# Seven block products in both layers' FFN, and one layer's modulation moved from VectorE to TensorE

## The chip, the cores and the metric

The kernel runs on one core of a Trainium2 chip. Its time is the device time of one execution in microseconds (us); 1701.05 is the median of three runs (1700.99 to 1702.76). The profile comes from one more execution, of 1706.92 us.

## The reference

Two layers work on 512 latent tokens and 256 context tokens of width 1024, in fp32. Each layer modulates its normed input, projects it, runs four head groups side by side (gated spatial mixing, a bidirectional mLSTM, windowed attention, pooling), projects out, adds; then the same with a gated FFN of hidden width 2816. Context tokens are dropped after layer 0's FFN and the keys, values and states that layer 1 takes from them.

```python
def trunk_layer(x, ctx, c, c_ctx, ...):
    sh_a, sc_a, g_a, sh_f, sc_f, g_f = split(silu(c) @ w_mod + b_mod, 6)      # context: the same of c_ctx
    zx = modulate(rms_norm(x, norm_g[0]), sh_a, sc_a) @ w_in
    mix_x, mix_c = token_mixers(zx, zc, ...)
    x = x + g_a * rms_norm(mix_x @ w_out, norm_g[1])
    x = x + g_f * rms_norm(swiglu(modulate(rms_norm(x, norm_g[2]), sh_f, sc_f), w_ffn_in, w_ffn_out), norm_g[3])

def swiglu(h, w_in_, w_out_):
    gate, up = split(h @ w_in_, 2)
    return (silu(gate) * up) @ w_out_
```

## The kernel before

**Products in three matmuls.** Activations lie as 8 tiles of 128 features by tokens. Every fp32 operand is split into a high half (`split`, L401 to L409: a copy on ScalarE, L405) and a low half (a subtraction on VectorE or GpSimd, L406), and a product is three matmuls (`mac3`, L464 to L466): high by high, high by low, low by high.

**Weights.** `weights` (L411) takes one unit: a load of up to 512 KB on SyncE's queue into the ring `wr` (5 slots), then the split into `wh` and `wl` (5 slots each). A `wr` slot is free again when its last reader is done; a load waits in the queue for its slot, and later loads wait behind it.

**Order.** Python emits the program in order, and a list scheduler with a cost model sets each engine's own order at build time, earlier emitted work first. Some work is emitted a piece at a time: modulation pieces stand in a list `bg`, and each `weights` call adds `bg_rate` to an account and emits a piece when it reaches 1 (`tick`); `flush` emits what is left.

**Modulation.** A layer has six parts of 1024 by 1024. `mods` (L603) does a part in four pieces of two row blocks: it loads two raw tiles of 512 KB into `wr`, runs four matmuls (each two instructions, L628) whose stationary operand is 128 x 32, each into another group of 32 columns of the array, and adds the result into a row buffer (VectorE, L631, L634); four transposes (L639) end a part. `mods_sums` (L653) does the same for latent tokens alone as weighted sums over rows on VectorE (L669, L671) into `macc`, and eight small matmuls with a vector of ones per half part (L677). Layer 0's parts 2 to 5 go by `mods` in layer 0's input projection, layer 1's parts 0 and 1 by `mods` during the context's FFN, and layer 1's parts 2 to 5 by `mods_sums` during layer 0's FFN (L1904).

**FFN.** The hidden width is 22 blocks of 128. A pair is block j of the gate and of the up weights; a chunk of pairs gives activations `g` (`gh`, `gl`), which an output tile per 128 features (`ffn_tiles`, L1602) multiplies by its block of `w_ffn_out` and adds to `y` (L1450). The first three pairs and the last output tiles run in two halves of 256 tokens, so that norms can overlap. Layer 0 (`ffn`, L1665) does all pairs dense: 2 x 8 matmul triples of 512 tokens. Layer 1 (`ffn_seven`, L1611) does 4 pairs dense and 18 by seven block products (Strassen's scheme in Winograd's form): the input's four quarters give sums (`strassen_rhs`, L1507), the pair's weights as a 2 by 2 block matrix give sums in the ring `ws` (`strassen_pair`, L1535, sums at L1547), and seven products of 4 triples with 256 tokens each, summed on the way out of PSUM, give gate and up. The output tiles of one chunk are emitted between the products of the next.

**Around it.** After layer 0's first three pairs, the context's states are computed, and the arena slots of the context are given to the latent tokens (`mix` in `run`). Layer 1's input projection is emitted by `order` from the string `l1`: first `in_halves`, then tiles between steps of the mLSTM (`m`), then attention (`a`).

Of the kernel before, what the change touches and what calls it, by code (L numbers as in the profile page):

```python
# [11 lines left out]
F32 = mybir.dt.float32  # L12
# [5 lines left out]
ALU = mybir.AluOpType  # L18
# [3 lines left out]
P = 128  # L22
D = 1024
KT = D // P
# [12 lines left out]
T = {'ntmp': 5,  # L37
 'netmp': 3,
 'nmain': 36,
 'nctx': 26,  # L40
 'wr': 5,
 'wh': 5,
 'wl': 5,
 'fcx': ((0, 8), (8, 15), (15, 22)),
 'fcc': ((0, 4), (4, 8), (8, 12), (12, 16), (16, 19), (19, 22)),
# [18 lines left out]
 'latei': 2,  # L64
 'rate0': 0.8,
 'rate1': 0.2,
 'rate2': 0.5,
 'lo': ('4', '4', '6', '3', '2', '4', '5', '3', '4'),
 'sqk': 'VPVPVPVP',
 'sqe': 'AAAAAAAA',  # L70
# [35 lines left out]
 'cbc': 's',  # L106
 'pom': '2310',
 'por': '1023',
 'strassen': (1,),
 'fcs': ((0, 4), (4, 8), (8, 12), (12, 15), (15, 22)),  # L110
 'sad': 'PPVV',
 'slo': 'PVVPPVP',
 'sre': 'VPVP',
# [1 line left out]
 'srl': 'VPVP',  # L115
 'sup': 'V',
 'sgl': 'V',
 'ws': 6}
UNIT = 1024
HALF = 544  # L120
NEG = -1e30
# [139 lines left out]
class Build:  # L261
    def __init__(self, tc, es, I, out, dbg=None):
        self.tc, self.nc, self.I, self.out, self.dbg = tc, tc.nc, I, out, dbg
        pool = lambda name, **k: es.enter_context(tc.tile_pool(name=name, **k))
        self.cp = pool("const", bufs=1)
        self.pp = pool("param", bufs=1)
        self.sp = pool("small", bufs=1)
        self.wr = pool("wr", bufs=T["wr"])
        self.wh = pool("wh", bufs=T["wh"])
        self.wl = pool("wl", bufs=T["wl"])  # L270
        self.ws = pool("ws", bufs=T["ws"])
        self.ap = pool("arena", bufs=1)
        self.dr = pool("dram", bufs=1, space=bass.MemoryType.DRAM)
        self.pmm = pool("pmm", bufs=4, space=PSUM)
        self.pmx = pool("pmx", bufs=3, space=PSUM)
        self.pms = pool("pms", bufs=1, space=PSUM)
        self.main = Arena(self.ap, "m", T["nmain"])
        self.side = Arena(self.ap, "c", T["nctx"])
        self.main.other, self.side.other = self.side, self.main
        self.tmp = Arena(self.ap, "t", T["ntmp"])  # L280
        self.etmp = Arena(self.ap, "e", T["netmp"])
        self.ar = self.main
        self.modrow = Arena(self.sp, "modrow", 1)
        self.bg = deque()
        self.pre = deque()
        self.bg_rate = self.bg_acc = 0.0
        self.uid = 0
        self.fine = False
        self.ph = 0
        self.lo_i = 0  # L290
        self.cpy_i = 0
# [116 lines left out]
            nc.scalar.activation(hi, src, AF.Copy, scale=scale)  # L408
            nc.vector.scalar_tensor_tensor(out=lo, in0=src, scalar=scale, in1=hi.bitcast(F32), op0=ALU.mult, op1=ALU.subtract)  # L409

    def weights(self, src, shape, hold=False):  # L411

        nc = self.nc
        if self.pre:
            return self.pre.popleft()
        self.tick()
        nk, m = shape
        raw = self.wr.tile([P, UNIT], F32, tag="wr", name=self.name("wr"))
        nc.sync.dma_start(out=raw[:, 0:nk * m].rearrange("p (a b) -> p a b", a=nk), in_=src)
        w = Stream()  # L420
        w.h, w.l, w.slots = [], [], []
        per = max(1, HALF // m)
        for a in range(0, nk, per):
            k = min(per, nk - a)
            if hold:
                w.slots += [self.ar.get("wt", F32R), self.ar.get("wt", F32R)]
                hi, lo = w.slots[-2].t, w.slots[-1].t
            else:
                hi = self.wh.tile([P, HALF], F32R, tag="wh", name=self.name("wh"))
                lo = self.wl.tile([P, HALF], F32R, tag="wl", name=self.name("wl"))  # L430
            self.lo_i += 1
            self.split(hi[:, 0:k * m], lo[:, 0:k * m], raw[:, a * m:(a + k) * m], eng=nc.gpsimd if self.lo_pool() else None)
            w.h += [hi[:, i * m:(i + 1) * m] for i in range(k)]
            w.l += [lo[:, i * m:(i + 1) * m] for i in range(k)]
        w.free = lambda: [x.free() for x in w.slots]
        return w
# [166 lines left out]
    def mods(self, l, parts, p, ahead=False):  # L603
# [44 lines left out]
        for part in parts:  # L648
            box = []
            for k0 in range(0, KT, 2):  # L650
                self.bg.append(lambda part=part, k0=k0, box=box: pair(part, k0, box))

    def mods_sums(self, l, parts, p, streams):  # L653

        nc = self.nc
        p.mod = getattr(p, "mod", None) or self.pp.tile([P, 48, 2], F32, tag=f"mod{l}", name=f"mod{l}")

        def pair(part, i, k0, acc):
            raw = self.wr.tile([P, UNIT], F32, tag="wr", name=self.name("wr"))
            c = slice(i * 512, i * 512 + 512)  # L660
            nc.sync.dma_start(out=raw.rearrange("p (k c) -> p k c", k=2), in_=self.I["wmod"][l, part, k0:k0 + 2, :, c].rearrange("k p c -> p k c"))
            if k0 == 0:
                acc += [self.main.get("macc") for _ in range(streams)]
            for k in (k0, k0 + 1):
                w = raw[:, (k - k0) * 512:(k - k0) * 512 + 512]
                for s in range(streams):
                    t = acc[s].t[:, 0:512]
                    if k == 0:
                        nc.vector.tensor_scalar(out=t, in0=w, scalar1=self.cs[:, k, s:s + 1], scalar2=1.0, op0=ALU.mult, op1=ALU.mult)  # L669
                    else:  # L670
                        nc.vector.scalar_tensor_tensor(out=t, in0=w, scalar=self.cs[:, k, s:s + 1], in1=t, op0=ALU.mult, op1=ALU.add)  # L671
            if k0 < KT - 2:
                return
            ps = self.ms()
            for s in range(streams):
                for b in range(4):
                    nc.tensor.matmul(ps[:, s * 4 + b:s * 4 + b + 1], acc[s].t[:, b * P:(b + 1) * P], self.ones[:, 0:1], start=True, stop=True)  # L677
                acc[s].free()
            o = part * 8 + i * 4
            for s in range(streams):  # L680
                nc.vector.tensor_tensor(out=p.mod[:, o:o + 4, s], in0=ps[:, s * 4:s * 4 + 4], in1=p.bmod[:, o:o + 4], op=ALU.add)

        for part in parts:
            for i in range(2):
                acc = []
                for k0 in range(0, KT, 2):
                    self.bg.append(lambda part=part, i=i, k0=k0, acc=acc: pair(part, i, k0, acc))

    def mod_col(self, p, l, s, kind):

# [844 lines left out]
    def strassen_pair(self, l, j, h, rhs, g, jj):  # L1535

        nc = self.nc
        n = h.half
# [4 lines left out]
            nc.sync.dma_start(out=r.rearrange("p (a b) -> p a b", a=KT), in_=self.I["wfi"][l, j, u])  # L1543
            raw.append(r)
        a11, a12, a21, a22 = raw[0][:, 0:512], raw[0][:, 512:1024], raw[1][:, 0:512], raw[1][:, 512:1024]
        s = [self.ws.tile([P, 512], F32, tag="ws", name=self.name("ws")) for _ in range(4)]
        tt = lambda c, o, a, b, op: self.e(c).tensor_tensor(out=o, in0=a, in1=b, op=op)  # L1547
        ad = T["sad"]
        tt(ad[0], s[0], a21, a22, ALU.add)
        tt(ad[1], s[2], a11, a21, ALU.subtract)  # L1550
        tt(ad[2], s[1], s[0], a11, ALU.subtract)
        tt(ad[3], s[3], a12, s[1], ALU.subtract)
        lhs = [a11, a12, s[1], s[0], s[2], s[3], a22]
        z, w, y = self.mm(), None, None
        c1 = self.ar.temp("fc", 2 * n)
        c2 = self.ar.temp("fd", n)
# [3 lines left out]
        for i in range(7):  # L1560
# [2 lines left out]
            self.split(hi, lo, lhs[i], eng=self.e(T["slo"][i]))  # L1563
            if i == 1:
                y = self.mm()
            if i == 3:
                w = self.mm()
            ps, first = [(z, True), (y, True), (z, False), (w, True), (z, False), (w, False), (z, False)][i]
# [33 lines left out]
    def ffn_tiles(self, l, y, g, j0, j1, whole, n, sq, first, end, ring):  # L1602

        for m in range(whole):
            w = self.weights(*self.ffo(l, m, j0, j1))
            ps = ring()
            self.dense(ps[:, 0:n], w, g, 0, n, nk=j1 - j0)
            self.evac_y(y, m, ps[:, 0:n], 0, n, sq, first, end)
            yield

    def ffn_seven(self, l, st, h, G, chunks, first, hold, last, hold2, then, between, after):  # L1611
# [29 lines left out]
        sums, rhs = self.strassen_rhs(h)  # L1641
        y = F32T(self.ar, "y", KT, n)
        for ci, (k0, k1) in enumerate(rest):
            gn = HL(self.ar, "g", k1 - k0, n)
            outs = self.ffn_tiles(l, y, g, j0, j1, KT, n, sq, ci == 0, False, self.mx)
            total, done = 7 * (k1 - k0), 0
            for i, _ in enumerate(self.strassen_tiles(l, k0, k1, h, rhs, gn)):
                while done * total < (i + 1) * KT:
                    next(outs)
                    done += 1  # L1650
            self.all(outs)
            g.free()
            g, j0, j1 = gn, k0, k1
# [162 lines left out]
    def run(self):  # L1816
# [81 lines left out]
        def mix():  # L1898
            self.ar = side
            self.ctx_states(C, pn)  # L1900
            main.absorb(side)
            main.other, self.tmp.lends = self.tmp, True
            self.ar = main
            self.mods_sums(1, (2, 4, 3, 5), pn, 1)  # L1904
            self.bg_rate = T["rate2"]

        self.layer_end(0, X, p, pn, norm, proj, mix)
        p = pn
# [1 line left out]
        self.drop_x(X)  # L1910
        X.m0 = C.mend
        self.ph = 5
        self.order(T["l1"], 1, X, C, hx, p, self.ring(T["r1"]), {})
        for s in C.ak_slots:
            s.free()
        C.av.free()
        self.layer_end(1, X, p)

    def layer_end(self, l, X, p, pn=None, norm=None, proj=None, mix=None):
# [150 lines left out]
```

## Time and profile before

| | before |
|---|---|
| median of three runs | 1701.05 us |
| profiled execution | 1706.92 us |
| its span, first to last instruction | 1705.1 us |
| TensorE busy | 94% |
| VectorE busy | 65% |
| ScalarE, GpSimd busy | 46%, 44% |
| mean granted TensorE clock | 0.967 of 2.4 GHz |

In a row, PE is TensorE's matmuls and PEld its weight loads, DVE VectorE, ACT ScalarE, POOL GpSimd and SP SyncE; a name with q is the engine's queue. `x18` is a count. A matmul's own duration overlaps its neighbours', so matmuls are counted by the distance of their starts. Tiles of latent tokens end in `_m`, of the context in `_c`.

### The profile page before, as it was taken

What the parts mean: (1) busy time and instruction counts of PE and PEld (TensorE: products, weight loads), DVE (VectorE), ACT (ScalarE), POOL (GpSimd) and SP (SyncE); (2) the same over time, 40 slices, a digit from 0 to 9 for tenths busy, and PEclk for the clock granted to TensorE, in tenths of its full rate; (3) what the DMA queues carried; (4) which work ended last, traced back from release to release, by engine and by line L of the source; (5) the groups of instructions that cost most, each with busy time, mean ns of one, the idle gap of its engine ahead of it and who ended that gap; (6) DMA issues with size and microseconds to landing.
All of it is one profiled execution on the core that took longest, in us unless ns stands there. A gap on an engine that the chain in (4) does not pass through costs nothing. (4 is left out here: it accounts for less than half of the span.)

```text
span 1705.1 us, 28934 instructions
## 1 busy us (share of the span) xinstructions
PE 1606.2 (94%) x10631; PEld 1403.3 (82%) x10631; DVE 1109.2 (65%) x2326; ACT 790.4 (46%) x1774; POOL 745.9 (44%) x775
## 2 busy tenths in 40 slices
PE   6999998998999999999999997999698989999997
PEld 2977777887899898888888887999478979998887
DVE  4976676758785668542444457658756867877774
ACT  3755356654345555233322334564564445544441
POOL 2421334454466554422222226233326766666653
PEclk9999999899999999999999998999699999999998
DMA  9654653354375323444444452121041223332241
GB/s 322 215 161 168 198 189 115 109 174 155 122 247 179 120 88 100 149 143 132 144 136 143 139 179 90 58 77 51 1 137 69 69 93 94 100 115 79 88 149 53
DMA packets 85662, 219.41 MB, mean 129 GB/s; under 512 B 11024, under 2 KB 20112, under 8 KB 85520
## 3 DMA queue, kind: packets, MB, share of 16 engines
q1 hardware_dynamic: 85520, 217.57, 39.3%
q8 instruction: 83, 1.36, 0.3%
q14 instruction: 59, 0.48, 0.1%
HBM read 211.24 MB, written 6.29 MB: 128 GB/s over the span
## 5 line engine op out<-in xcount | busy, mean ns | idle before, releaser
L406 POOL TENSOR_TENSOR wl<-wr,wh 128x512 fp32r<-128x512 f32 (+2 forms) x248 | 335.1, 1357 | 498.3 <-ACT wh L405 464.0
L405 ACT ACTIVATE wh<-wr 128x512 fp32r<-128x512 f32 (+2 forms) x508 | 308.9, 617 | 465.1 <-PE mm L465 328.4
L406 DVE TENSOR_TENSOR wl<-wr,wh 128x512 fp32r<-128x512 f32 (+3 forms) x260 | 214.8, 829 | 120.0 <-ACT wh L405 117.4
L464 PE MATMUL mm<-hfh_m,wh 128*128 128x512 f32 (+1 forms) x320 | 124.8, 390 | 0.0
L466 PE MATMUL mm<-hfh_m,wl 128*128 128x512 f32 (+1 forms) x320 | 124.4, 389 | 0.0
L465 PE MATMUL mm<-hfl_m,wh 128*128 128x512 f32 (+1 forms) x320 | 124.1, 388 | 0.0
L465 PE MATMUL mm<-hfl_c,wh 128*128 128x256 f32 x352 | 100.5, 286 | 0.6 <-POOL hfl_c L576 0.6
L466 PE MATMUL mm<-hfh_c,wl 128*128 128x256 f32 x352 | 100.1, 285 | 0.0
L464 PE MATMUL mm<-hfh_c,wh 128*128 128x256 f32 x352 | 99.7, 284 | 0.0
L405 ACT ACTIVATE wh<-ws 128x512 fp32r<-128x512 f32 x72 | 45.1, 630 | 60.3 <-PE mm L465 33.3
L466 PEld LDWEIGHTS mm<-hfh_m,wl 128*128 128x128 f32 x320 | 60.1, 188 | 13.5
L465 PEld LDWEIGHTS mm<-hfl_m,wh 128*128 128x128 f32 x320 | 60.2, 188 | 13.0
L464 PEld LDWEIGHTS mm<-hfh_m,wh 128*128 128x128 f32 x320 | 60.2, 188 | 12.9
L464 PEld LDWEIGHTS mm<-hfh_c,wh 128*128 128x128 f32 x352 | 66.2, 188 | 5.3 <-issue 2.3
L465 PEld LDWEIGHTS mm<-hfl_c,wh 128*128 128x128 f32 x352 | 66.4, 189 | 1.9 <-POOL hfl_c L576 1.0
L466 PEld LDWEIGHTS mm<-hfh_c,wl 128*128 128x128 f32 x352 | 66.4, 189 | 1.5 <-issue 0.6
L406 POOL TENSOR_TENSOR wl<-ws,wh 128x512 fp32r<-128x512 f32 x36 | 59.7, 1673 | 17.7 <-ACT wh L405 17.6
L671 DVE SCALAR_TENSOR_TENSOR macc_m<-wr,cs,macc_m 128x512 f32<-128x512 f32 x56 | 44.9, 802 | 29.7 <-DMA wr<-in_wmod_dram 28.6
L464 PE MATMUL mm<-gh_m,wh 128*128 128x512 f32 x155 | 61.3, 398 | 2.1 <-ACT wh L405 1.5
L465 PE MATMUL mm<-gl_m,wh 128*128 128x512 f32 x155 | 61.0, 394 | 0.0
L466 PE MATMUL mm<-gh_m,wl 128*128 128x512 f32 x155 | 60.9, 394 | 0.0
L465 PE MATMUL mx<-gl_m,wh 128*128 128x512 f32 x120 | 48.0, 400 | 6.2 <-DVE gl_m L409 4.8
(722 smaller groups left out, 5443.5 us busy)
## 6 DMA issues: line engine op xcount, KB each, us to landing
wr<-in_wfi_dram SPq DMA_DIRECT2D x132, 512.0 KB, 3.7
wr<-in_wmod_dram SPq DMA_DIRECT2D x80, 512.0 KB, 3.8
wr<-in_wT_dram SPq DMA_DIRECT2D x42, 512.0 KB, 3.8
wr<-in_wo_dram SPq DMA_DIRECT2D x24, 512.0 KB, 3.7
wr<-in_wfo_dram SPq DMA_DIRECT2D x24, 512.0 KB, 3.9
wr<-in_wfo_dram SPq DMA_DIRECT2D x24, 448.0 KB, 3.9
wm_m<-in_wmod_dram SPq DMA_DIRECT2D x32, 256.0 KB, 5.3
wr<-in_wfo_dram SPq DMA_DIRECT2D x24, 256.0 KB, 2.7
```

What stands on the lines that cost most here:

```text
L405: nc.scalar.activation(hi, src, AF.Copy)
L406: (eng or nc.vector).tensor_tensor(out=lo, in0=src, in1=hi.bitcast(F32), op=ALU.subtract)
L464: nc.tensor.matmul(out, lh, rh, start=first, stop=False, skip_group_check=more)
L465: nc.tensor.matmul(out, lh, rl, start=False, stop=False, skip_group_check=more)
L466: nc.tensor.matmul(out, ll, rh, start=False, stop=last, skip_group_check=more)
L671: nc.vector.scalar_tensor_tensor(out=t, in0=w, scalar=self.cs[:, k, s:s + 1], in1=t, op0=ALU.mult, op1=ALU.add)
```

## The change

- Layer 0's FFN goes by `ffn_seven` too (`strassen`).
- Both layers' chunks become 4, 3, 4, 5 and 6 blocks (`fcs`); they were 4, 4, 4, 3, 7 in layer 1 and 8, 7, 7 in layer 0. The first four output tiles of the first chunk are emitted ahead of the first product (`fco`).
- Output weights of all chunks but the last load into a ring of their own, `wq` (2 slots of 640 columns), and no longer into `wr`.
- A pair keeps two of its four weight sums in `ws` (4 slots, were 6); the other two are written over the raw tiles, the last one after the second product's split.
- `mods_sums` goes. Layer 1's parts 2 to 5 go by `mods`, emitted a piece at a time (`rate2` 0.8 a weight unit) from the start of layer 1's `order`, with a `flush` after it.

```diff
- 'rate2': 0.5,
+ 'rate2': 0.8,
- 'strassen': (1,),
- 'fcs': ((0, 4), (4, 8), (8, 12), (12, 15), (15, 22)),
+ 'strassen': (0, 1),
+ 'fcs': ((0, 4), (4, 7), (7, 11), (11, 16), (16, 22)),
+ 'fco': 4,
+ 'wq': 2,
- 'ws': 6}
+ 'ws': 4}
...
-    def weights(self, src, shape, hold=False):
+    def weights(self, src, shape, hold=False, ring=None):
...
-        raw = self.wr.tile([P, UNIT], F32, tag="wr", name=self.name("wr"))
+        if ring:
+            raw = ring.tile([P, 5 * P], F32, tag="wq", name=self.name("wq"))
+        else:
+            raw = self.wr.tile([P, UNIT], F32, tag="wr", name=self.name("wr"))
...
-    def mods_sums(self, l, parts, p, streams):
...
     def strassen_pair(self, l, j, h, rhs, g, jj):
...
-        s = [self.ws.tile([P, 512], F32, tag="ws", name=self.name("ws")) for _ in range(4)]
+        s1, s2 = (self.ws.tile([P, 512], F32, tag="ws", name=self.name("ws")) for _ in range(2))
...
-        tt(ad[0], s[0], a21, a22, ALU.add)
-        tt(ad[1], s[2], a11, a21, ALU.subtract)
-        tt(ad[2], s[1], s[0], a11, ALU.subtract)
-        tt(ad[3], s[3], a12, s[1], ALU.subtract)
-        lhs = [a11, a12, s[1], s[0], s[2], s[3], a22]
+        tt(ad[0], s1, a21, a22, ALU.add)
+        tt(ad[1], a21, a11, a21, ALU.subtract)
+        tt(ad[2], s2, s1, a11, ALU.subtract)
+        lhs = [a11, a12, s2, s1, a21, a12, a22]
...
             if i == 1:
                 y = self.mm()
+                tt(ad[3], a12, a12, s2, ALU.subtract)
...
-            w = self.weights(*self.ffo(l, m, j0, j1))
+            w = self.weights(*self.ffo(l, m, j0, j1), ring=None if end else self.wq)
...
         for ci, (k0, k1) in enumerate(rest):
+            outs = self.ffn_tiles(l, y, g, j0, j1, KT, n, sq, ci == 0, False, self.mx)
+            ahead = 0 if ci else T["fco"]
+            for _ in range(ahead):
+                next(outs)
             gn = HL(self.ar, "g", k1 - k0, n)
-            outs = self.ffn_tiles(l, y, g, j0, j1, KT, n, sq, ci == 0, False, self.mx)
...
-                while done * total < (i + 1) * KT:
+                while done * total < (i + 1) * (KT - ahead):
...
-            self.mods_sums(1, (2, 4, 3, 5), pn, 1)
-            self.bg_rate = T["rate2"]
...
         self.ph = 5
+        self.mods(1, (2, 4, 3, 5), pn)
+        self.bg_rate = T["rate2"]
         self.order(T["l1"], 1, X, C, hx, p, self.ring(T["r1"]), {})
...
+        self.flush()
         self.layer_end(1, X, p)
```

## Rows read from the trace of the kernel before

**Rows 1.** The page: span, TensorE's busy time, and bytes moved in 40 equal slices.

```profile
span 1705.1 us, 28934 instructions
...
PE 1606.2 (94%) x10631; PEld 1403.3 (82%) x10631; DVE 1109.2 (65%) x2326; ACT 790.4 (46%) x1774; POOL 745.9 (44%) x775
...
GB/s 322 215 161 168 198 189 115 109 174 155 122 247 179 120 88 100 149 143 132 144 136 143 139 179 90 58 77 51 1 137 69 69 93 94 100 115 79 88 149 53
```

**Rows 2.** Stretches: length, busy us (instructions) by engine, granted clock, DMA share, GB/s.

```profile
724.70:1005.00 280.30, 280.30 (x1240) 228.45 (x1239) 125.18 (x181) 89.21 (x152) 67.60 (x51) 1.00 0.44 147
1005.00:1057.00 52.00, 42.30 (x309) 41.01 (x308) 26.31 (x52) 16.72 (x38) 22.96 (x35) 0.89 0.33 109
1057.00:1188.50 131.50, 131.02 (x1050) 126.30 (x1049) 92.75 (x270) 72.00 (x174) 42.86 (x67) 0.99 0.20 62
1188.50:1265.00 76.50, 60.32 (x362) 43.34 (x360) 55.47 (x189) 44.56 (x136) 26.86 (x35) 0.82 0.17 55
1364.20:1643.40 279.20, 263.67 (x1824) 244.16 (x1823) 206.64 (x249) 134.35 (x252) 178.01 (x122) 0.98 0.32 99
```

**Rows 3.** TensorE's waits, layer 1's products: waiter, releaser, us in total, times, longest.

```profile
PE mx L465 <- DVE gl_m L409: 4.8, 1, 4.8
...
PE mm L466 <- POOL wl L406: 2.7, 3, 1.6
```

**Rows 4.** GpSimd's waits in the same stretch.

```profile
POOL ws L1547 <- DMA wr<-in_wfi_dram: 47.4, 15, 5.6
```

**Rows 5.** Waits of SyncE's queue in the same stretch.

```profile
SPq L1543 <- POOL wl L406: 86.5, 23, 12.1
```

**Rows 6.** Timeline of TensorE, layer 0's FFN: start, duration, instruction.

```profile
899.74 0.40 PE L465 MATMUL mm<-gl_m,wh 128*128 128x512 f32 x1
...
911.80 0.40 PE L466 MATMUL mm<-gh_m,wl 128*128 128x512 f32 x1
```

**Rows 7.** Timeline of TensorE, one block product of layer 1.

```profile
1506.88 0.28 PE L464 MATMUL mm<-st0h_m,wh 128*128 128x256 f32 x1
...
1508.18 0.28 PE L466 MATMUL mm<-st0h_m,wl 128*128 128x256 f32 x1
```

**Rows 8.** The page's groups: TensorE's weight loads (count, busy us, mean ns, idle before).

```profile
L464 PEld LDWEIGHTS mm<-hfh_m,wh 128*128 128x128 f32 x320 | 60.2, 188 | 12.9
```

**Rows 9.** Timeline of TensorE at the last of the weighted sums.

```profile
1034.44 0.95 PE L677 MATMUL ms<-ones,macc_m 128*128 128x1 f32 x8
1035.25 0.69 PE L559 MATMUL mx<-ident,rmsy 128*128 128x128 f32 x4
```

**Rows 10.** VectorE's groups by line in 724.7 to 1005.

```profile
L671 DVE SCALAR_TENSOR_TENSOR macc_m<-wr,cs,macc_m 128x512 f32<-128x512 f32 x48 | 38.8, 809 | 27.4 <-DMA wr<-in_wmod_dram 26.4
```

**Rows 11.** TensorE's waits in 1005 to 1057, the tail of layer 0's FFN.

```profile
PE ms L548 <- DVE sq_t L523: 7.2, 1, 7.2
```

**Rows 12.** Timeline of TensorE, one pair of layer 0's modulation.

```profile
165.67 0.39 PE L466 MATMUL mm<-hxh_m,wl 128*128 128x512 f32 x1
165.99 1.07 PE L628 MATMUL ms<-wr,cs 128*32 128x512 f32 x8
166.98 0.39 PE L464 MATMUL mm<-wh,hxh_m 128*128 128x272 f32 x1
```

**Rows 13.** Timeline of TensorE, the transposes of one part.

```profile
490.30 0.60 PE L639 MATMUL ms<-ident,modrow_modrow 128*128 128x128 f32 x4
490.65 0.36 PE L466 MATMUL mm<-hfh_c,wl 128*128 128x256 f32 x1
```

**Rows 14.** TensorE's waits in 1185 to 1265, layer 1's mixers.

```profile
PE mx L1425 <- DVE ht_m L794: 7.8, 3, 3.4
```

**Rows 15.** One source line: durations in ns (least/median/most), first and last start.

```profile
L634 DVE TENSOR_TENSOR modrow_modrow<-ms,modrow_modrow x18: 658/688/692, 120.0 to 487.3; 128x512 f32<-128x512 f32 x18
```

**Rows 16.** The line of the low halves, in 1380 to 1643.

```profile
L406 POOL TENSOR_TENSOR wl<-ws,wh x34: 1292/1740/1755, 1391.0 to 1641.8; 128x512 fp32r<-128x512 f32 x34
L406 DVE TENSOR_TENSOR wl<-ws,wh x33: 674/693/1773, 1386.4 to 1635.6; 128x512 fp32r<-128x512 f32 x33
```

More of the change, by code (lines that the diff above doesn't have):

```diff
@@ L271, in __init__ @@
         self.ws = pool("ws", bufs=T["ws"])
+        self.wq = pool("wq", bufs=T["wq"])
         self.ap = pool("arena", bufs=1)
@@ L651, in mods @@
                 self.bg.append(lambda part=part, k0=k0, box=box: pair(part, k0, box))
-    def mods_sums(self, l, parts, p, streams):
[L655 to L687, printed above, removed]
     def mod_col(self, p, l, s, kind):
```

## The prediction

> **What bounds the kernel now.** Read first the page's busy shares: TensorE is busy 94% of the span, every other engine at most 65% [rows 1]. So the question for each part is whether it takes work from TensorE, adds some, or makes it wait; the other engines count where TensorE waits for them. The stretches by stage come next [rows 2]. In the dense body of layer 0's FFN (724.7 to 1005) TensorE is busy 280.3 of 280.3 us and VectorE 125: each matmul taken out there shortens the span by its full spacing. Layer 1's input projection (1057 to 1188.5) is as full, 131.0 of 131.5. The rest of its mixers (1188.5 to 1265) is not: 16.2 us idle, at a granted clock of 0.82. Layer 1's FFN, which uses seven block products already, is the model for the new layer 0 (1364.2 to 1643.4): 15.5 us idle, granted clock 0.98, VectorE busy 207 and GpSimd 178 of 279 us. A mean of 0.98 with 1.2 and 2.4 GHz as levels means some 4% of the stretch, 11 us, at the lower one, worth 5.6 us; so 21 us are lost there. Counted from spacings (below) it is 279.2 − 261.9 = 17. I take 19.
>
> The waits of TensorE in that stretch tell why [rows 3]: 4.8 us once, at its start, for the gate of the last dense pair, and pieces of 1 to 2 us for `wl`, the low halves. Behind those stands GpSimd, which waited 47.4 us for raw FFN weights to land before it could form the sums of the next pair [rows 4], and the issue of these loads waited 86.5 us in the queue for a slot of `wr`, which GpSimd's last subtraction gives back [rows 5].
>
> **The change part by part.**
>
> *Block products in layer 0.* In the stretch of full-width matmuls, the first and last of 53 in succession start at 899.74 and 911.80: 12.06/52 = 0.232 us each [rows 6]. In layer 1's products the first and last of 12 half-width ones start at 1506.88 and 1508.18: 1.30/11 = 0.118 [rows 7]. A dense pair is 2 × 8 × 3 = 48 full-width matmuls, 11.14 us; a pair by seven products is 7 × 4 × 3 = 84 half-width ones, 9.91 us. 18 of the 22 pairs change: 18 × 1.22 = **−22.0 us**. Pair j=3 stays dense but reads its input in quarters, 96 × 0.118 instead of 11.14: **+0.2**. The output products are 22 × 8 × 3 matmuls however chunked. (The 261.9 above is 18 × 9.91 + 15 × 8 × 3 × 0.232.)
>
> The Trainium skill, page "TensorE: Matmul & The Clock Gate", section "Back-to-back issue gap", gives a sustained stream of weight load and matmul about 131 ns at 512 columns and 81 at 128; halving the width would then save less than half, and an estimate by its straight line (98 at 256) makes a pair 8.2 instead of 6.3 us, so 18 pairs 35 us slower. This trace disagrees: 232 and 118 ns, almost the ratio of the widths.
>
> What layer 0's products lose again: with layer 1 as model between 0 and 21 us, and the start of the stage shares VectorE with the context's states. Three edits work on the loss, in both layers. `fco` puts four output tiles (4 × 12 × 0.232 = 11 us) ahead of the first product, so the sums of the input have that long to be formed. The output weights leave `wr` for `wq`, so that all five `wr` slots serve pairs, two each: the load for pair j+2 is asked for when pair j ends, a whole pair (14 us with its outputs) ahead of use, where a landing takes under 6 [rows 4]. In return both raw tiles of a pair are held to products 6 and 7, because differences are now written into them; the extra half pair pays for that. And `ws` 4 for 2 sums a pair, instead of 6 for 4, lets the next pair's sums start a pair ahead. What none of them removes is the chain copy, subtraction, matmul itself, the 1 to 2 us pieces. I take 9 us lost per layer, about half of today's: **+9** in layer 0, 9 − 19 = **−10** in layer 1. Bounds: 2 (waits gone) and 24 (today's and the context's) per layer.
>
> *The weighted sums go.* In layer 0 the sums over rows were 8 groups of 8 small matmuls; such a group holds TensorE from 1034.44 to 1035.25 [rows 9]: 8 × 0.81 = **−6.5 us**, in a stage that is full. VectorE loses 48 updates of 0.81 us in the dense body alone, 38.8 us, and 27.4 us of waiting in its queue ahead of them [rows 10]: this makes room for the products' work, and is worth nothing by itself, as TensorE did not wait there [rows 2].
>
> *The tail of layer 0's FFN.* TensorE waits 7.2 us there for the first half's norm [rows 11], with the second half's last chunk as cover. That chunk has now 6 blocks for 7: 6 tiles × 3 × 0.118 = **+2** us less cover (bounds 0 and 4). In layer 1 nothing follows, so there it is nothing.
>
> *Modulation on TensorE.* Four parts of four pairs, each pair 8 matmuls into four column groups at a time. One of layer 0 starts behind a matmul of 165.67 and the next begins at 166.98: 1.31 − 0.23 = 1.08 us [rows 12]. The four transposes of a part take 490.30 to 490.65 [rows 13]. So 16 × 1.08 + 4 × 0.35 = 18.7 us of TensorE. Where: 17 weight units of the projection count 0.8 each, so 13 pairs fall among its tiles, which leave no room, and 3 go behind the mixers, into idle time. The 13 cost 14 and three transposes 1. Against it, the mixers' chains (scan, then attention) get those 15 us of wall time earlier, and TensorE waited 7.8 us for the scan's output there [rows 14]; I let 2 come back: **+13**. Bounds: 4, if the gaps take nearly all, and 20, if nothing comes back and VectorE's 16 further operations of 0.69 us [rows 15] delay the attention. Its 32 loads of 512 KB enter the one queue between the projection's: what stands behind a load that waits for a slot is the next tile's weights. The stretch moved 62 GB/s [rows 2]; 16.8 MB more in 131 us make 190. Layer 0's projection, which carries the same loads already, moved 161 to 199 (slices 3 to 6) [rows 1], so I hold them hidden; if they were not, each late pair would cost up to a landing, under 6 us [rows 4].
>
> **Sum**, against the profiled execution (1706.9 us, span 1705.1): −22.0 + 0.2 + 9 − 10 − 6.5 + 2 + 13 = −14.3. The median shown is 1701.05, 5.9 below that execution; I carry the difference over: **1686.8 us**.
>
> **The rivals.**
>
> *A, slower: VectorE and GpSimd set the pace of the products.* Their subtractions stretch each other: the same one is 0.69 us at its median and 1.77 at most on VectorE, 1.74 at its median on GpSimd, where 1.29 is the shortest [rows 16]. The Trainium skill, "GPSIMD Engine Reference", section "8. Key points", says that GpSimd shares its SBUF interfaces with VectorE, and that instructions with two SBUF inputs contend; by that rule the pair of engines is nearer its limit than the busy shares show, and the trace agrees. Per pair GpSimd has 6 such operations, up to 10.4 us, and VectorE 207/18 = 11.5 [rows 2]; TensorE with its outputs 262/18 = 14.5. It decides once the stretched work passes 14.5 per pair, which layer 1 does not show as a whole; but its first pairs also carry the input's sums, and in layer 0 the context's states. Then both layers lose 24: −22 + 0.2 + 24 + 5 − 6.5 + 2 + 19 (modulation late as well) = +21.7, some **1723**; halfway, 1710.
>
> *B, a wash: the waits of layer 1 stay* (rings were not their cause) and layer 0 loses 9, modulation pays in full: −22 + 0.2 + 9 + 0 − 6.5 + 2 + 18.7 = +1.4, **1702**.
>
> *C, better: the loads were the cause*, waits all but go (4 a layer) and most of the modulation fits the gaps: −22 + 0.2 + 4 − 15 − 6.5 + 2 + 4 = −33, **1668**.
>
> *D, half-width matmuls wait for their weight loads:* a load is 188 ns [rows 8]; were it not hidden, a pair would be 84 × 0.188 = 15.8 us, 18 × 4.7 = +84 instead of −22, and the time about **1793**. Rows 7 show 118 with a load for each; 1 in 100.
>
> **How the numbers follow.** Forecast (1676 to 1697) 0.50, A (over 1705) 0.17, B (1697 to 1705) 0.12, C (under 1676) 0.20, D 0.01. 0.2%, about what a measurement of this kernel tells from no change, is 3.4 us: 1697.6 to 1704.5. Faster 0.72, within 0.08, slower 0.20. The range for 8 in 10 takes in C and B: **1664 to 1706**.
>
> **What would show it.** Right: layer 0's FFN has rows `st0` to `st3` and its products and outputs, from the fourth dense pair to the last chunk, take some 295 us; no `macc`; `wmod` matmuls of 1.1 us a pair between the projection's tiles and that projection some 15 us longer; GpSimd's 47.4 us for raw weights down to a few; the 4.8 at the start gone. Wrong: a `wl` or `ws` wait of several us per pair in layer 0 (A), layer 1's FFN as long as before (B), the projection lengthened by under 6 us (C).

## The result and the profile after

| | before | after |
|---|---|---|
| median (4 runs each, same chip) | 1701.9 us | 1719.72 us |
| lowest to highest | 1700.99 to 1704.39 | 1714.26 to 1723.3 |
| span of the profiled execution | 1705.1 us | 1721.5 us |

The ratio is 1.0084 [1.0064, 1.0104]: slower by 0.84%, some 14 us, where 1686.8 us, 14.3 less than before, were forecast. (The two medians alone differ by 17.8 us, 1.05%; the text goes by the ratios.) The page: TensorE's busy time is 10 us more than in [rows 1], its idle time 6 us more. The time is not in one place.

```profile
span 1721.5 us, 31798 instructions
...
PE 1616.4 (94%) x11794; PEld 1443.4 (84%) x11794; DVE 1196.9 (70%) x2449; ACT 837.6 (49%) x1906; POOL 878.3 (51%) x866
```

The stretches of after, which answer to [rows 2] (columns as there): layer 0's products from the first output tile to the last chunk, the tail, layer 1's projection, its mixers, its products.

```profile
723.20:1016.30 293.10, 281.32 (x2345) 277.87 (x2344) 205.80 (x273) 141.50 (x281) 190.34 (x131) 1.00 0.33 104
1016.30:1061.50 45.20, 34.10 (x265) 33.35 (x263) 27.15 (x51) 16.31 (x36) 20.36 (x33) 0.87 0.37 118
1061.50:1220.70 159.20, 157.79 (x1179) 133.79 (x1179) 108.40 (x312) 72.51 (x175) 45.12 (x69) 0.97 0.41 137
1220.70:1290.40 69.70, 57.84 (x366) 37.88 (x364) 56.47 (x185) 44.15 (x134) 24.03 (x31) 0.93 0.34 111
1389.80:1684.40 294.60, 284.89 (x1952) 261.00 (x1951) 211.89 (x276) 143.69 (x283) 189.75 (x133) 1.00 0.33 101
```

The projection is as full as before, but 28 us longer; the mixers are 7 shorter. In layer 0's products TensorE is idle for 11.8 us, with VectorE and GpSimd at 206 and 190 us of 293.

Cut at the same instructions in every kernel (layer 0's FFN from its first matmul to the projection's first, the projection up to the first attention matmul, and so on), the profiled executions come to, in us:

| kernel | layer 0's FFN | projection | mixers | out-proj. | layer 1's FFN | span |
|---|---|---|---|---|---|---|
| before | 410.5 | 131.3 | 76.3 | 45.7 | 394.6 | 1705.1 |
| after | 413.2 | 159.2 | 69.7 | 48.3 | 382.8 | 1721.5 |
| e1, layer 0 dense | 401.6 | 156.2 | 70.7 | 45.3 | 387.7 | 1710.0 |
| e3, dense and weighted sums | 411.6 | 131.3 | 76.4 | 45.8 | 387.5 | 1700.9 |
| e4, no modulation | 414.4 | 131.5 | 74.3 | 49.7 | 385.5 | 1701.8 |
| e8, modulation in the mixers | 408.6 | 140.2 | 76.1 | 49.8 | 386.9 | 1707.6 |

What lies ahead of these, 644 to 650 us, is the same work in all. The front of layer 0's FFN, from its first matmul to its first output tile, scatters from 71 to 82 us between kernels that share that code, its products' stretch by 1.3 us (293.1 in after, 292.7 in e4, 291.8 in e8); so sums are taken from the ratios, and places from the spans.

Layer 0's products run at the spacing that was counted on: the first and last of 12 half-width matmuls, answering to [rows 7], are 1.30 us apart, 0.118 each.

```profile
802.01 0.28 PE L470 MATMUL mm<-st2h_m,wh 128*128 128x256 f32 x1
...
803.31 0.28 PE L472 MATMUL mm<-st2h_m,wl 128*128 128x256 f32 x1
```

TensorE's waits in that stretch: pieces for `wl`, as in [rows 3], and some for `fd_m`, VectorE's step between two products. Those that the profile lists are short and few.

```profile
PE mm L470 <- DVE fd_m L1551: 3.2, 5, 1.3
PE mx L494 <- POOL wl L409: 2.6, 2, 1.7
PE mm L472 <- POOL wl L409: 2.2, 2, 1.5
```

In layer 1's products (1389.8 to 1684.4) TensorE's 4.8 us for the gate are gone, and of 6.7 us for `wl` (the 2.7 of [rows 3], 1.0 more for GpSimd and 3.0 for VectorE) 1.1 are left; those for `fd_m` rose from 2.0 to 3.6. GpSimd's wait for raw weights, which answers to [rows 4], has fallen from 47.4 to 17.9 us:

```profile
POOL ws L1517 <- DMA wr<-in_wfi_dram: 17.9, 13, 2.8
```

In layer 0's products VectorE stands long behind GpSimd's sum:

```profile
DVE ws L1517 <- POOL ws L1517: 41.6, 15, 5.3
```

### The profile page after: what moved, and what is told of

It is laid out like the page before. It is cut to its first block, busy times and chain, and to the rows that moved or that the text cites. A ratio compares the mean times of both kernels' runs of the same rounds, so it can differ in the third digit from the quotient of the medians.

```text
span 1721.5 us, 31798 instructions
## 1 busy us (share of the span) xinstructions
PE 1616.4 (94%) x11794; PEld 1443.4 (84%) x11794; DVE 1196.9 (70%) x2449; ACT 837.6 (49%) x1906; POOL 878.3 (51%) x866
## 4 chain that ended last, share of the span: by engine, by line
PE 71%; DVE 14%; DMA 5%; issue 4%; POOL 3%; ACT 3%; SPq 0%; DVEq 0%; POOLq 0%; ACTq 0%
PE mm L470 15%; PE mm L472 15%; PE mm L471 15%; PE ms L634 3%; DVE wl L409 2%; PE mx L1111 2%; POOL wl L409 2%; PE mx L492 1%; PE mx L494 1%; PE mx L493 1%; PE mx L472 1%; PE mx L471 1%; PE mx L470 1%; PE mx L1105 1%; PE ms L554 1%
## 5 line engine op out<-in xcount | busy, mean ns | idle before, releaser
L1517 DVE TENSOR_TENSOR ws<-ws,wr 128x512 f32<-128x512 f32 x36 | 51.9, 1441 | 69.9 <-POOL ws L1517 69.9
L494 PE MATMUL mx<-gh_m,wl 128*128 128x256 f32 x256 | 72.2, 282 | 3.8 <-POOL wl L409 2.6
L492 PE MATMUL mx<-gh_m,wh 128*128 128x256 f32 x256 | 71.8, 282 | 1.2 <-ACT gh_m L408 1.2
L493 PE MATMUL mx<-gl_m,wh 128*128 128x256 f32 x256 | 71.8, 281 | 0.0
L1517 POOL TENSOR_TENSOR ws<-wr 128x512 f32<-128x512 f32 x36 | 47.3, 1313 | 48.1 <-DMA wr<-in_wfi_dram 46.9
L408 ACT ACTIVATE wh<-wq 128x512 fp32r<-128x512 f32 (+1 forms) x80 | 42.9, 541 | 44.6 <-PE mm L471 19.0
L409 POOL TENSOR_TENSOR wl<-wq,wh 128x512 fp32r<-128x512 f32 (+1 forms) x40 | 57.4, 1435 | 12.1 <-ACT wh L408 8.2
L1517 POOL TENSOR_TENSOR wr<-wr,wr 128x512 f32<-128x512 f32 x36 | 60.8, 1689 | 1.0
L634 PE MATMUL ms<-wr,cs 128*32 128x512 f32 x320 | 57.3, 614 | 0.0
L470 PE MATMUL mx<-gh_m,wh 128*128 128x512 f32 x128 | 50.6, 398 | 2.3 <-ACT wh L408 1.6
```

What stands on the lines that cost most here:

```text
L408: nc.scalar.activation(hi, src, AF.Copy)
L409: (eng or nc.vector).tensor_tensor(out=lo, in0=src, in1=hi.bitcast(F32), op=ALU.subtract)
L470: nc.tensor.matmul(out, lh, rh, start=first, stop=False, skip_group_check=more)
L492: nc.tensor.matmul(out[:, c], w.h[w0 + i], ah[:, c], start=f and q == 0, stop=False)
L493: nc.tensor.matmul(out[:, c], w.h[w0 + i], al[:, c], start=False, stop=False)
L494: nc.tensor.matmul(out[:, c], w.l[w0 + i], ah[:, c], start=False, stop=z and q == 1)
```

## The experiments

Every ratio is to the kernel before on the same chip. Without another word the edits are to the changed kernel.

### The three parts one at a time

**e1: layer 0's FFN dense.**

```diff
- 'strassen': (0, 1),
+ 'strassen': (1,),
```

> The changed kernel with layer 0's FFN dense as before; layer 1's chunks and rings and the modulation on TensorE stay. The two traces put layer 0's FFN 2.7 us longer with the products than without. Theory 1 (the stage gives back, at its front and in its body, all that the fewer matmuls save): 3 us less than the changed kernel, some 1717. Rival (the products save the 18 us forecast, and something else in the program lengthened that stretch): 1735 or more.

1712.68 us, 1.0044 [1.0029, 1.0059]: between the kernel before and the changed one, 0.40% or 7 us under the latter (11.5 in the profiled executions), where theory 1 said 3. The products of layer 0 cost time as they stand.

**e2: the weighted sums on VectorE, beside layer 0's products.**

```diff
- 'rate2': 0.8,
+ 'rate2': 0.5,
+    def mods_sums(self, l, parts, p, streams):
...
+            self.mods_sums(1, (2, 4, 3, 5), pn, 1)
...
-        self.mods(1, (2, 4, 3, 5), pn)
```

> The changed kernel with layer 1's parts 2 to 5 as weighted sums on VectorE during layer 0's FFN, as before; products in both layers stay. Theory 1 (modulation on TensorE costs 24 us in layer 1, not 13): 24 less in layer 1, and 6.5 of matmuls plus 0 to 8 us of VectorE's contention more in layer 0: 1702 to 1710. Rival (the sums can't run beside the products: VectorE becomes the pace): layer 0's FFN 25 us or more longer, 1720 or more.

1750.38 us, 1.0263 [1.0246, 1.028]. Layer 0's FFN takes 460.3 us, 47 more than after. Its body, to the last chunk (stretch of e2):

```profile
644.70:1057.40 412.70, 374.98 (x2887) 364.40 (x2886) 322.13 (x452) 169.86 (x344) 244.96 (x179) 0.94 0.40 131
```

VectorE is busy 322 of 413 us and TensorE idle 38, as the rival said. With both on VectorE the stage is 47 us longer; this is what the move to TensorE avoids.

**e3: e2's edit and e1's, which is the kernel before with the new rings and chunks of layer 1.**

> The kernel before with only the chunks, rings and weight sums of layer 1's FFN changed. Theory 1: layer 1's FFN 12 us shorter and nothing else moves: 1690. Rival (that gain came with the other edits): 1702.

1699.42 us, 0.997 [0.996, 0.998]. With e1 and after this is a chain: rings and chunks −0.30%, modulation in place of weighted sums +0.74%, layer 0's products +0.40%: −5, +12.6 and +6.8 us of 1705. They add up to the whole 0.84% because each is the difference of two neighbours; by the intervals, the last is 6.8 ± 4, and the one before it 12.6 ± 3.

**e4: layer 1's modulation parts 2 to 5 left out (the bias alone).**

```diff
-        self.mods(1, (2, 4, 3, 5), pn)
-        self.bg_rate = T["rate2"]
+        nc.vector.tensor_copy(pn.mod[:, 16:48, 0], pn.bmod[:, 16:48])
```

> The changed kernel without the modulation of layer 1's parts 2 to 5 (they are the bias alone; that part is left out). Theory 1: layer 1 from its projection to its FFN takes 24 us less, the 253 of before: 1696. Rival (the matmuls cost the 13 forecast and the rest is the order of the work): 1707.

1703.62 us, 0.9991 [0.9976, 1.0005], 0.93% or 16 us under after: nearer the rival's 13 than theory 1's 24. The projection is back at 131.5; by the stretches of the table the modulation costs 27.7 − 4.6 − 1.4 = 21.7 us.

### Where layer 0's products lose

**e5: no weight sums in either layer; the products take unsummed blocks.**

```diff
-        tt(ad[0], s1, a21, a22, ALU.add)
-        tt(ad[1], a21, a11, a21, ALU.subtract)
-        tt(ad[2], s2, s1, a11, ALU.subtract)
-        lhs = [a11, a12, s2, s1, a21, a12, a22]
+        lhs = [a11, a12, a22, a21, a21, a12, a22]
...
-                tt(ad[3], a12, a12, s2, ALU.subtract)
```

> The changed kernel without the four sums of a pair's weights, in both layers (the products take raw blocks in their place; that part of the computation is left out). Going from dense to products costs layer 0's FFN 12.8 us where the fewer matmuls should save 22; the bodies of the two stages lose some 18 and 15 us. Theory 1 (GpSimd, VectorE and ScalarE wait for one another in their queues over the sums, and TensorE for the last of them): both bodies lose 5 or less without them, some 22 us less in all, 1697 where the changed kernel is 1719. Rival (the low halves, or the reading of PSUM between products, hold TensorE whatever the sums): under 6 us less, 1713 or more.

1694.13 us, 0.9937 [0.9915, 0.996]. Layer 0's products take 277.8 us for 293.1, layer 1's body 282.4 for 294.6. The stretch of layer 0 in e5:

```profile
720.60:998.40 277.80, 277.29 (x2344) 276.87 (x2343) 151.55 (x237) 146.41 (x280) 129.53 (x99) 1.00 0.35 109
```

TensorE is idle 0.5 us, and 2344 matmuls at 0.118 are 277: nothing is lost any more.

**e6: no sums of the input's quarters in layer 0.**

```diff
+    def plain_rhs(self, h):
+        (b11, b12), (b21, b22) = h.blocks
+        return [], [b11, b21, b12, b11, b22, b22, b21]
...
-        sums, rhs = self.strassen_rhs(h)
+        sums, rhs = self.strassen_rhs(h) if l else self.plain_rhs(h)
```

> The changed kernel without the sums of the input's quarters in layer 0 (products take the quarters themselves; that part is left out). Theory 1 (these sums share VectorE with the gates and the context's states, and the front loses 9 us to that): 8 to 10 us less, 1710. Rival (the front is slow for the context's states alone): within 2 us of the changed kernel, 1717 to 1721.

1716.75 us, 1.006 [1.0037, 1.0082], 4 us under after, which the two intervals don't tell from nothing; 7.5 in the profiled execution's FFN, all ahead of the products. The stretches of e6, from the first FFN matmul to the first output tile and then to the last chunk:

```profile
648.20:715.60 67.40, 64.38 (x481) 59.77 (x481) 45.11 (x96) 24.57 (x59) 32.49 (x40) 0.95 0.34 106
715.60:1008.70 293.10, 283.24 (x2342) 279.42 (x2341) 200.56 (x266) 139.04 (x276) 181.92 (x127) 0.99 0.34 104
```

The first was 74.9 us in after; the second is the same 293.1. The 67.4 is lower than the front of every kernel that forms these sums (71 to 82), but the size is uncertain, as the front scatters.

**e7: 512-wide output tiles in layer 0.** The output matmuls ran in two halves of 256 because a flag was left set by the context's keys, which the dense FFN resets and the new path does not.

```diff
+        self.fine = False
         sums, rhs = self.strassen_rhs(h)
```

> The changed kernel with layer 0's output products 512 tokens wide; in the changed kernel they run as two of 256, left so by a flag that the context's keys set. Theory 1: 384 x (2 x 0.118 - 0.232) = 1.5 us, 2 with the waits: 1717. Rival (the doubled weight loads explain why layer 0's body loses more than layer 1's): 4 us or more, 1715 or less.

1713.41 us, 1.0035 [1.0022, 1.0048]. The products take 286.9 for 293.1. 416 full-width in place of 832 half-width matmuls would by the spacings save 98.2 − 96.5 = 1.7; the rest is less waiting. Whether the doubled weight loads make that waiting, as the rival has it, is not shown.

**e9: e7, and the first weight sum on VectorE.**

```diff
- 'sad': 'PPVV',
+ 'sad': 'VPVV',
```

> The changed kernel with layer 0's output products 512 wide and the first of a pair's four weight sums on VectorE instead of GpSimd, in both layers. Without the sums layer 0's body was 15 and layer 1's 12 us shorter. Theory 1a (it is the order in the queues: VectorE waited 42 us in layer 0's body for GpSimd's first sums): each body 4 us or more shorter than with wide outputs alone, some 1702 where that kernel is 1711 and the changed one 1719. Rival (it is the amount of work, two engines slowing each other): within 3 us of the kernel with wide outputs, 1708 to 1714.

1710.38 us, 1.0028 [1.0005, 1.0052]. The products' stretch in e9:

```profile
729.50:1014.60 285.10, 277.38 (x1928) 256.77 (x1928) 207.29 (x283) 141.17 (x279) 159.98 (x113) 1.00 0.33 103
```

285.1 us, 1.8 less than e7. VectorE now waits 47.6 us for the raw weights at that sum where it waited 41.6 for GpSimd: that wait, or the order of the two engines, was the cause of some 2 us at most, as the rival said.

```profile
DVE ws L1517 <- DMA wr<-in_wfi_dram: 47.6, 16, 4.9
```

**e13 and e14: one engine's two sums left out.** The lines of e5 with GpSimd's two kept (e13), or with VectorE's two kept (e14).

```diff
-        lhs = [a11, a12, s2, s1, a21, a12, a22]
+        lhs = [a11, a12, a22, s1, a21, a12, a22]    # e13
+        lhs = [a11, a12, s2, a22, a21, a12, a22]    # e14, s2 = a21 - a11
```

> The changed kernel with only GpSimd's two weight sums of a pair formed; the two of VectorE are left out, and the products that took them take unsummed blocks. Without all four sums layer 0's products after the first took 277.8 us instead of 293.1 and layer 1's body 282.4 instead of 294.6. Theory (the sums cost by their amount, on whichever of the two engines): about half of it comes back, layer 0 some 285, layer 1 some 288, ratio about 1.001. Rival (GpSimd's slow sums at the head of each pair gate the products, VectorE's don't): under 4 us come back in each, layer 0 over 289, layer 1 over 291, ratio 1.005 or more.

> The changed kernel with only VectorE's two weight sums of a pair formed; GpSimd's two are left out, and the products that took them take unsummed blocks. Theory (amount): about half comes back, layer 0's products after the first some 285, layer 1's body some 288, ratio about 1.001. Rival (GpSimd's sums gate): nearly all comes back, layer 0 under 280, layer 1 under 285, ratio 0.995 or less.

1691.28 us, 0.9918 [0.9894, 0.9942], and 1693.54 us, 0.9929 [0.9911, 0.9948]. Theory and rival both fell: leaving out either half brings nearly all of it back (e14 alone is as its rival said, but e13 speaks against that rival). The products' stretch in e13, then in e14:

```profile
719.00:996.70 277.70, 277.04 (x2345) 276.84 (x2345) 169.38 (x239) 145.81 (x281) 178.29 (x131) 1.00 0.35 109
```

```profile
721.70:1000.40 278.70, 277.39 (x2344) 276.78 (x2343) 180.15 (x271) 145.93 (x280) 133.27 (x99) 1.00 0.35 109
```

TensorE has some 1 us of idle time in either, so the loss is not a price per sum. Nor is a long wait for the raw weights its cause: in e14 VectorE waits 42.3 us for them at its first sum, and TensorE loses nothing by it.

```profile
DVE ws L1517 <- DMA wr<-in_wfi_dram: 42.3, 16, 3.5
```

The groups of low halves in that stretch (count, busy us, mean ns), first after, then e14, show why one engine's relief is also the other's: 36 subtractions on VectorE took 42.9 us with GpSimd's sums about, and 29.7 without.

```profile
L409 DVE TENSOR_TENSOR wl<-wr,wh 128x512 fp32r<-128x512 f32 x36 | 42.9, 1191 | 12.1 <-ACT wh L408 11.8
```

```profile
L409 DVE TENSOR_TENSOR wl<-wr,wh 128x512 fp32r<-128x512 f32 x36 | 29.7, 825 | 14.8 <-ACT wh L408 13.3
```

**e16, e17, e18: work moved from VectorE to GpSimd, nothing left out.** All on e7 with e8's modulation (below).

```diff
- 'slo': 'PVVPPVP',
+ 'slo': 'PVPPPVP',    # e16; e17 with 'sup': 'P' as well
+ 'slo': 'PVVPPPP',    # e18
```

> The changed kernel with 512-wide outputs in layer 0 and the modulation's pairs spread into the mixers (as in the kernel with all mends), GpSimd keeping both its weight sums, and one of VectorE's three low halves a pair (the third product's) given to GpSimd. Theory (VectorE's load sets the loss: with 206 us of work beside 190 on GpSimd 12 us were lost, with 169 beside 178 none, with 207 beside 160 13): VectorE falls to some 188 and GpSimd goes to some 215; layer 0's products after the first 278 us or less where 286.9 stood, layer 1's body 288 or less where 298.7 stood with the same modulation; ratio about 0.988. Rival (the work of both engines together sets it, 396 us before and now some 403): layer 0 285 or more, layer 1 294 or more, ratio 0.995 or more.

> The kernel before this one with the product of gate and up (the last 256-wide multiplication of a pair, 18 in a layer, 0.97 us each on VectorE) on GpSimd as well. Theory (VectorE's load): a little better still or the same, layer 0 276 or less, ratio 0.986 to 0.990. Rival (both together, GpSimd now the fuller one at some 235 us): layer 0 288 or more, ratio 0.996 or more.

> The first kernel of these three with another low half given to GpSimd, the sixth product's (of the block that the fourth sum is written over) in place of the third's: the same amount of work at another place in the queues. Theory (load): within 2 us of the first kernel in both layers. Rival (place: the third product's low stands behind GpSimd's two sums, the sixth's doesn't): this one is better by 5 us or more in a layer, or worse by as much.

1709.67 us, 1.0026 [1.0012, 1.0041]; 1703.5 us, 0.9982 [0.9966, 0.9999]; 1708.56 us, 1.0022 [1.0005, 1.0039]. The products of layer 0 take 288.6, 284.7 and 289.9 us, layer 1's body 302.4, 298.2 and 294.3. The theory of VectorE alone fell. e16 is as its rival said (the work of both engines together), but e17, with still more of that work, loses less. The products' stretch in e17, VectorE 194 and GpSimd 236, then in e18, 193 and 212:

```profile
724.60:1009.30 284.70, 278.53 (x1929) 257.10 (x1928) 194.04 (x233) 142.18 (x280) 235.89 (x167) 1.00 0.33 104
```

```profile
716.10:1006.00 289.90, 280.27 (x1928) 257.45 (x1927) 193.09 (x252) 140.14 (x280) 211.71 (x149) 1.00 0.33 103
```

Place decided something in layer 1 (e18 is 8 us better than e16 in its body, and 5 worse behind it), not in layer 0.

### The modulation elsewhere, and better versions

**e8: half the rate in the projection, the rest emitted after the mixers' scan.**

```diff
- 'rate2': 0.8,
+ 'rate2': 0.4,
- 'l1': '... p9 u1 h a1 m1 P ...',
+ 'l1': '... p9 u1 h F a1 m1 P ...',    # F is flush
```

> The changed kernel with the modulation's pieces at 0.4 a weight unit in the projection (6 of 16 pairs) and the other ten emitted ahead of the attention. Theory 1 (the projection has no room on TensorE, the mixers had 16 us of it): projection 10 pairs x 1.5 = 15 us shorter, mixers 7 longer: 1711. Rival (the mixers are a chain through VectorE that these pieces lengthen by as much): 1718 or more.

1712.31 us, 1.0035 [1.0021, 1.0049]. The projection falls by 19 us and the mixers rise by 6.4.

**e10 to e12 and e15:** e10 is e3 with e9's sum, e11 is e7, e8 and e9's sum, e12 is e1, e8 and e9's sum, e15 is e12 at rate 0.2.

> The kernel before with layer 1's new chunks and rings and the first weight sum on VectorE: 0.997 of the kernel before without that sum. Theory 1a: layer 1's body 4 us shorter, 0.995. Rival: 0.997.

> Products in both layers, outputs 512 wide, first weight sum on VectorE, ten modulation pairs in the mixers. If the parts add: 1719 - 8 (outputs) - 10 (mixers) - 8 (sum) = 1693 by theory 1a, 0.993 of the kernel before; by its rival 1701, 0.998.

> As the last, with layer 0's FFN dense. The products of layer 0, mended, then cost 6 us less 4 for the sum against dense: 2 us below the last kernel by theory 1a, 1691; by the rival, which leaves layer 0's products 6 us dearer than dense, 1695.

> Layer 0's FFN dense, the first weight sum on VectorE, and the modulation's pairs at half the earlier rate in the projection (0.2 a weight unit), the rest emitted after the mixers' scan. At 0.4 the projection took 144.3 us and the mixers 76.3, ratio 0.9939. Theory (a piece among the projection's tiles costs its full 1 us or more, one in the mixers half of that): about 3 pieces leave the projection, 140 us or less there, mixers 78, ratio about 0.993. Rival (the pieces that are left pile up behind the scan and hold the attention): mixers 82 or more, ratio 0.995 or more.

| kernel | median us | ratio to before |
|---|---|---|
| e10 | 1698.84 | 0.9951 [0.9934, 0.9968] |
| e11 | 1695.75 | 0.9943 [0.992, 0.9967] |
| e12 | 1697.71 | 0.9939 [0.9921, 0.9958] |
| e15 | 1700.81 | 0.9975 [0.9956, 0.9993] |

All beat both kernels; e10 to e12 can't be told apart. e15's projection took 138.6 us and its mixers 79.3, against 144.3 and 76.3 in e12, a little less than e12 in sum, which its median does not show. With products in both layers (e11) or dense in layer 0 (e12) the time is the same: mended, layer 0's products save about what they lose, and no more.

## Why the prediction was wrong

By the chain of e3, e1 and after, the sum's terms stand so, in us:

| term | forecast | measured |
|---|---|---|
| layer 1's FFN | −10 | −5 (stretches −7 to −12) |
| weighted sums gone, modulation on TensorE | −6.5 + 13 | +12.6 |
| layer 0's products, their loss, the tail | −22 + 0.2 + 9 + 2 | +6.8 |

**The step that failed is "What layer 0's products lose again": +9, with 24 as its upper bound.** The gain itself was right: 0.118 us a matmul, and in e5 and e13 the stretch holds nothing but its matmuls. So 6.8 = −21.8 + loss, and the loss is 28.6, the tail's included, uncertain by 4 like the 6.8 (by the medians alone it would be some 3 more). Of it e13 shows 15.4 as waits that the weight sums make, e6 4 to 7.5 as the input's sums ahead of the first product, and e7's flag makes 1.7 in matmuls beside the waits that it shares with the sums; 4.3 are the tail's (below). That leaves up to 3, within the uncertainty.

**The reason given was wrong in a telling way.** The prediction read [rows 4] and [rows 5] as the cause of the waits and let the new rings cure half. The rings did what was said of them: the wait for raw weights fell to 17.9 us, the 4.8 went. What TensorE loses stayed for the most part: from the first output tile to the last whole one, layer 1's body took 300.9 us in before, 298.1 in e3 and 294.6 in after, which have the same products there, and e5 takes 12.2 more out of it by leaving the weight sums out. The view of [rows 3] had a sign of this that the prediction passed over: waits for VectorE's low halves and for `fd_m`, longer together than those for GpSimd.

```profile
PE mx L466 <- DVE wl L406: 3.0, 2, 1.9
...
PE mm L464 <- DVE fd_m L1581: 2.0, 1, 2.0
```

Busy time of the two engines in layer 0's products, with the loss against the matmuls' own time (277.7, with 512-wide outputs some 276 by the spacings):

| kernel | VectorE | GpSimd | loss |
|---|---|---|---|
| after | 206 | 190 | 15.4 |
| e7 | 206 | 189 | 11 |
| e9 | 207 | 160 | 9 |
| e11 | 208 | 162 | 8.5 |
| e16 | 203 | 220 | 13 |
| e17 | 194 | 236 | 9 |
| e18 | 193 | 212 | 14 |
| e13 | 169 | 178 | 0 |
| e14 | 180 | 133 | 1 |

None of the ways of sharing the same work that ran removes the loss (8.5 to 15.4 us), and taking either half of the sums away removes all but 1. That points to rival A's mechanism, the two engines setting the pace, at a lower point than its own: in after VectorE works 206/18 = 11.4 and GpSimd 10.6 us a pair, under the 14.5 from which A said that it decides. Rival A's time, 1723, is close to the result, and so are its terms for layer 0 (−22 + 0.2 + 24 + 2 = +4.2 for +6.8) and for the sums and the modulation (−6.5 + 19 for +12.6); but it had layer 1 lose 5 where it gained. Of its sign, several us a pair for `wl` or `ws`, TensorE's waits show little (6.1 us for `wl` in all 18 pairs); VectorE's `ws` wait is there, 2.3 a pair, and e9 shows that little hangs on it.

**What stays open** is what sets this point. The amount of work alone does not order the losses: e17 has more of it than e18 (430 us on both engines for 405) and loses 9 where e18 loses 14. e13 and e14 lessen the work and also cut a chain (third sum from first, fourth from third; e14 cuts the first link alone). e9 has the whole work with both ends of that first link on one engine, and still loses 9. No run had the full work without the chain, so whether the amount, the chain or the places in the queues decide is not shown.

**The modulation: +13 forecast, about 19 measured** (e1's projection, mixers and out-projection against e3's, 24.9 − 5.7 − 0.5; by e4 16 by the ratios and 22 in the stretches). The pair's price of 1.08 was right, but not the count. The 13 pairs in the projection run as 19 pieces, each an unbroken run of their matmul instructions, since the order puts other work between a pair's instructions; and a piece of two costs as much as a whole pair. TensorE's timeline, answering to [rows 12]: the piece of two holds it from 1091.54 to 1092.51, 0.97 us, that of six from 1093.18 to 1094.17, 0.99.

```profile
1091.21 0.40 PE L499 MATMUL mm<-hxl_m,wt_m 128*128 128x256 f32 x2
1091.54 1.04 PE L634 MATMUL ms<-wr,cs 128*32 128x512 f32 x2
1092.51 0.74 PE L499 MATMUL mm<-hxl_m,wt_m 128*128 128x256 f32 x4
1093.18 1.06 PE L634 MATMUL ms<-wr,cs 128*32 128x512 f32 x6
1094.17 0.39 PE L470 MATMUL mm<-hxh_m,wt_m 128*128 128x256 f32 x1
```

The 19 pieces take 19.9 us by their starts where 14 were counted. A whole pair of eight, for comparison:

```profile
1119.07 1.06 PE L634 MATMUL ms<-wr,cs 128*32 128x512 f32 x8
1120.06 0.38 PE L492 MATMUL mm<-hxh_m,wh 128*128 128x256 f32 x1
```

The Trainium skill, "TensorEngine Tiling (Array Packing)", section "Key Properties", says that a change of the tiling mode, not of the tile alone, drains TensorE. The trace agrees in that a piece costs about 1 us whatever is in it (0.97 us with two instructions, 0.99 with eight); a drain itself is not to be seen in it.

The other 8 us of the projection are 12 transposes and 14 matmuls of the mixers that moved into it, and a lower granted clock: e1's projection, the same work at 0.99 where after has 0.97, takes 156.2 us, 3 less. Of the mixers 6.6 us came back, where 2 were taken: the wait for the scan's output fell from the 7.8 of [rows 14] to 2.8. The bound of 4 for "the gaps take nearly all" fell, as 13 of 16 pairs never met a gap; e8, which sends ten pairs there, shows that the gaps do take them at a third of the price (19 us for 6.4). The 32 loads stayed hidden, as forecast: in the projection TensorE's one wait of over a microsecond is for ScalarE. (The 199 GB/s that the prediction compares with is 198 in [rows 1], which changes nothing.)

```profile
PE mx L1395 <- DVE ht_m L764: 2.8, 2, 1.6
```

**Right:** the weighted sums by their direction, −6.5 forecast and −6 to −10 measured (12.6 − 18.7 = −6.1; in the stretches layer 0's FFN is 411.6 us in e3 and 401.6 in e1); layer 1's FFN by its direction and, in the stretches, its size; that D does not hold, by the spacing. **The tail** cost about what was forecast, 2.6 for 2: its wait grew from the 7.2 of [rows 11] to 9.8 (in e7 and e13 as well). Against e1, which keeps the chunk of 7 and has no weighted sums either, it is 9.8 for 5.5, and these 4.3 are its part of the 28.6. The length of the stretch does not show it (49.2 us in before, 46.3 in e1, 45.2 in after), because the smaller chunk also moves matmuls out of it, into the products' stretch. The wait in after, then in e1:

```profile
PE ms L554 <- DVE sq_t L529: 9.8, 1, 9.8
```

```profile
PE ms L554 <- DVE sq_t L529: 5.5, 1, 5.5
```

## What to carry to other kernels

A product scheme that saves matmuls spends elementwise work, and the two engines that share that work can cost as much as the scheme saves, long before either looks full: here 206 and 190 of 293 us lost 15, and 169 and 178 lost nothing. Busy shares alone do not tell the loss (194 and 236 lost 9, 193 and 212 lost 14), so leave the work out on the chip and see what comes back. Do the same before a long wait is named the cause: the raw weights' wait was the smaller part of it, and VectorE's for GpSimd hardly any. Work that is hidden in a full stage costs its switches as well: count the pieces that the order will make of it, and send them where TensorE is idle.

## What the runs showed of the hardware that was not expected

Work on GpSimd lengthens VectorE's. Leaving out GpSimd's 32 sums of layer 0's products (e14) shortened VectorE's work there from 206 to 180 us at nearly the same count of instructions (273 and 271). The Trainium skill, "GPSIMD Engine Reference", section "8. Key points", says that the two share SBUF interfaces and contend where VectorE has two SBUF inputs; the trace agrees, with a mean of 825 ns for 1191 on the low halves.

Four column groups of 128 x 32 cost about 1 us a visit, with two instructions in it (0.97) or eight (0.99).
